# Two-layer encoder trunk: w_down sums beside the up projection, w_up sums closer together, last channel block reordered, weights, table load and transposes moved

## The chip, the cores and the metric

The kernel runs on one core of a Trainium2 chip. The metric is the device time of one execution in microseconds (us). Three runs of the kernel before gave 2811.72 to 2815.82 us, with a median of 2812.99. The core has five engines that run side by side and wait for each other through semaphores: TensorE (PE, matrix products), VectorE (DVE), ScalarE (ACT), GpSimd (POOL) and SyncE (SP), which issues most of the DMA transfers. DMAs with an addition on the way (accumulating ones) are issued by POOL.

## What is computed

Two layers (DEPTH = 2) over x of 1024 x 1024, float32. Cut to what matters:

```python
for l in range(DEPTH):
    h = rms_norm(x, mix_norm[l])
    x = x + hybrid_mixer(h, ...)            # 6 MLA heads, 6 GQA heads, gMLP; then @ w_out
    h = rms_norm(x, mem_x_norm[l])
    x = x + memory_cross_attention(h, mem, mem_kv_norm[l], mem_w_q[l], mem_w_kv[l], mem_w_o[l])
    h = rms_norm(x, ffn_norm[l])
    x = x + conv_gated_ffn(h, ffn_w_up[l], ffn_conv_w[l], ffn_conv_b[l], ffn_w_down[l])
return rms_norm(x, final_norm)

def conv_gated_ffn(h, w_up, conv_w, conv_b, w_down):
    a = h @ w_up                            # 1024 -> 2 x 2816
    a = depthwise_conv3(a) + conv_b         # over the tokens
    gate, val = a[..., :D_FF], a[..., D_FF:]
    return (silu(gate) * val) @ w_down
```

memory_cross_attention normalises mem (256 tokens), makes keys and values of it (4 heads of 128) and attends from all 1024 tokens.

## The kernel before, in words

Every float32 product is made of three fp32r products: both operands are split into a high part (rounded to fp32r) and the rest, and `mm3` adds high x high, high x low and low x high (L116, L117, L118). `load` (L106 to L111) fetches a weight block of 128 x 1024 (512 KB) by an SP DMA (L106), rounds it on POOL (L110, or on ACT at L108) and takes the rest on DVE (L111). `split` does the same to a product: ACT L123 and DVE L124, or with a scale L126 and L127. `transpose4` (L140) makes four 128 x 128 transposes on PE. Tiles of 4 KB per partition come from 46 slots `s`; a load is issued when the slot's earlier readers are done.

A layer is a sequence of stages: the input projection (weights w_m, w_kv, w_q, w_a), attention, the output projection w_out, the memory stage, the up projection and the down projection. Times of layer 0 in the trace: attention some 170 to 500 us, memory stage 590 to 700, up projection 710 to 1190, then down until 1400. Layer 1 stands some 1396 us later.

**Attention.** 24 items (12 heads x 2 halves of the tokens), each with four steps: scores on PE (L725, L726 for GQA, `mm3` for MLA), a maximum on DVE (L295), the exponential on ACT (L299), a division by the sum on POOL (L305), transposes on PE (L140) of what L305 wrote, values (L318, L319). The list `extra` hangs further work on an item. `fill` does so for small pieces of PE work.

**The sums.** Up and down projection are done as 2 x 2 block products with 7 instead of 8 products (numbers m = 1 to 7), for which four sums of blocks of each weight are needed (m = 5, 7, 6, 3). They are made in DRAM: `Blocks.copy` copies a piece by an SP DMA (L777, not before the last L305 issued so far), `Blocks.add` adds another piece to it by an accumulating DMA of POOL (L782). Sum 6 adds the finished sum 5 to its copy, sum 3 the finished sum 6. w_up has 6 pieces per sum (UP_PARTS: one of 0.5 MB and five of 1 MB, 23.1 MB in the 24 sums of a layer), w_down has 3 (768 KB and two of 1 MB, 11.5 MB in 12 sums). `u_6_4` is sum 6 of w_up, piece 4; `d_5_0` is sum 5 of w_down, piece 0.

The 24 w_up copies stand at items 0 to 19, each sum 4 items later; the 12 w_down copies stand at items 0 to 18. The 12 w_down sums are issued by `add_later`: one after each of the four heads of the memory keys (L945) and one in each of the nine score steps of the memory attention (L1031).

**Output projection and memory stage.** In the second half of the output projection (t = 0 to 7) each token block gets 24 `mm3` matmuls (`wo_bc`, `wo_a`). After t = 5 the normalised memory rows `mn` are turned by 16 transposes (`mT`). Then come the key weights mem_wk, the values mem_wv, the queries mem_wq with 8 score steps, and mem_wo.

**Up projection.** 22 channel blocks j, 7 products m each, in the order of the list `order` (L1054 to L1057). One product is 12 matmuls (L1123 to L1125). `fetch` issues the load of one 128 x 512 weight tile (256 KB, from in_w_up or a sum u) and `make_w` splits it (ACT L1076, DVE L1077); `fetch` runs FETCH = 9 and `make_w` AHEAD = 4 products before the product. `post` adds the results on DVE (L1143 to L1149; L1149 for m = 4). The gated blocks go to DRAM, where POOL sums them (L1196, g_u).

**Next layer.** `down` pops small steps from the list `todo`, which turn the next layer's normalised input. Layer 1's first weights w_m are loaded at the head of `layer`.

The order on each engine is the program's order where `tc.keep_in_program_order` asks for it, and otherwise that of a scheduler that may hoist instructions.

## Time and profile before

| what | value |
|---|---|
| median of three runs | 2812.99 us |
| profiled execution | 2817.39 us |
| its span | 2815.4 us |
| PE busy | 2742.6 us, 97% |
| DVE busy | 1971.9 us, 70% |
| ACT busy | 1469.9 us, 52% |
| POOL busy | 689.5 us, 24% |
| DMA of SP's queue (q1) | 323.84 MB, 34.3% of 16 engines' span |
| DMA of POOL's queue (q0) | 92.28 MB, 18.2% |

The span is what the profiler recorded between first and last instruction; the profiled execution's time holds 2 us around it. Busy shares are means over all stages. PE is the engine with the largest share, and its idle time is spread over many waits, so the views that list waits and stretches tell more than the shares. The mean granted clock of PE was 0.991 of the full one.

### The profile page before, as it was taken

To read this page: it belongs to the slowest core of one execution; us is meant where nothing else is said; L and a number is where in the kernel's file an instruction comes from. 1 tells how busy PE (TensorE), PEld (TensorE's weight loads), DVE (VectorE), ACT (ScalarE), POOL (GpSimd) and SP (SyncE) were. 2 spreads that over 40 slices of the span, in tenths; PEclk is the share of its full clock that TensorE was granted. 3 is DMA by queue.
4 is the path that set the end of the run, shared out by engine and by line. 5 is a ranking of instruction groups with operands and counts; after the bars stand their busy time and mean duration, and the time that the engine had idled before them with its cause. 6 is when DMAs were issued, how large, how long until landed. Compare 5 with 4: busy or idle time off the path is not lost.

```text
span 2815.4 us, 38016 instructions
## 1 busy us (share of the span) xinstructions
PE 2742.6 (97%) x13648; PEld 2299.2 (82%) x13648; DVE 1971.9 (70%) x2953; ACT 1469.9 (52%) x2836; POOL 689.5 (24%) x696
## 2 busy tenths in 40 slices
PE   9999999989999999999999999999899999999998
PEld 7987788777878888888889877878788788888887
DVE  5479889555597777774445798894566877777744
ACT  4378877223564444553333788872245544445432
POOL 3245666321100000000123356662210000000000
PEclk9999999999999999999999999999999999999999
DMA  4026886245246656785220269951651556657752
GB/s 145 26 76 178 224 220 154 75 120 128 83 124 170 175 164 176 219 269 185 86 62 19 78 186 247 224 140 53 150 121 66 146 169 176 168 171 239 247 187 104
DMA packets 160748, 418.80 MB, mean 149 GB/s; under 512 B 17840, under 2 KB 18480, under 8 KB 146224
## 3 DMA queue, kind: packets, MB, share of 16 engines
q1 hardware_dynamic: 137376, 323.84, 34.3%
q0 software_dynamic: 23040, 92.28, 18.2%
q8 instruction: 107, 1.75, 0.3%
q14 instruction: 81, 0.66, 0.1%
q10 hardware_dynamic: 144, 0.26, 0.0%
HBM read 371.75 MB, written 206.05 MB: 205 GB/s over the span
## 4 chain that ended last, share of the span: by engine, by line
PE 82%; DVE 7%; ACT 4%; DMA 3%; issue 2%; POOL 2%; SPq 0%; POOLq 0%; DVEq 0%; ACTq 0%
PE bank L1236 8%; PE bank L116 7%; PE bank L118 7%; PE bank L117 7%; PE pair L1236 6%; PE bank L140 6%; PE bank L1124 5%; PE bank L1125 5%; PE bank L1123 5%; PE pair L1123 4%; PE pair L1124 4%; PE pair L1125 4%; PE pair L116 2%; PE pair L118 2%; PE pair L117 2%
## 5 line engine op out<-in xcount | busy, mean ns | idle before, releaser
L116 PE MATMUL bank<-s,s 128*128 128x512 f32 (+4 forms) x1124 | 408.2, 364 | 13.3 <-DVE s L124 8.0
L118 PE MATMUL bank<-s,s 128*128 128x512 f32 (+4 forms) x1124 | 405.2, 361 | 5.5 <-DVE s L111 5.0
L124 DVE TENSOR_TENSOR s<-bank,s 128x512 fp32r<-128x512 f32 (+3 forms) x552 | 331.1, 629 | 107.8 <-ACT s L123 105.3
L117 PE MATMUL bank<-s,s 128*128 128x512 f32 (+4 forms) x1124 | 404.0, 359 | 0.0
L123 ACT ACTIVATE s<-bank 128x512 fp32r<-128x512 f32 (+3 forms) x552 | 285.9, 555 | 220.6 <-PE bank L140 135.3
L140 PE MATMUL bank<-ident,s 128*128 128x128 f32 (+1 forms) x2320 | 322.8, 275 | 26.8 <-DVE s L127 13.4
L140 PEld LDWEIGHTS bank<-ident,s 128*128 128x128 f32 (+1 forms) x2320 | 270.6, 140 | 84.7 <-DVE s L127 16.6
L305 POOL TENSOR_SCALAR s<-s,stat 128x1024 f32<-128x1024 f32 x192 | 226.0, 1178 | 221.6 <-DVE stat L304 156.7
L1076 ACT ACTIVATE s<-s 128x512 fp32r<-128x512 f32 x308 | 187.8, 627 | 168.6 <-PE bank L1125 49.8
L1124 PE MATMUL bank<-s,s 128*128 128x512 f32 x704 | 274.8, 390 | 0.7 <-DVE s L209 0.7
L1125 PE MATMUL bank<-s,s 128*128 128x512 f32 x704 | 274.2, 389 | 0.0
L1123 PE MATMUL bank<-s,s 128*128 128x512 f32 x704 | 274.0, 390 | 0.0
L295 DVE TENSOR_REDUCE stat<-pair 128x1 f32<-128x1024 f32 x192 | 233.7, 1217 | 44.3 <-PE pair L726 22.5
L116 PEld LDWEIGHTS bank<-s,s 128*128 128x128 f32 x1124 | 215.6, 192 | 42.9 <-DVE s L124 10.4
L1236 PE MATMUL bank<-s,s 128*128 128x512 f32 (+1 forms) x1068 | 242.7, 387 | 1.6 <-DVE stat L131 1.6
L132 POOL TENSOR_TENSOR stat<-stat,mhalf 128x1 f32<-128x1 f32 (+3 forms) x94 | 85.6, 911 | 643.6 <-DVE stat L131 642.0
L118 PEld LDWEIGHTS bank<-s,s 128*128 128x128 f32 x1124 | 216.8, 193 | 31.7 <-DVE s L111 5.4
L1221 DVE TENSOR_TENSOR s<-s,s 128x512 fp32r<-128x512 f32 x264 | 170.6, 685 | 95.4 <-ACT s L1220 95.0
L117 PEld LDWEIGHTS bank<-s,s 128*128 128x128 f32 x1124 | 216.8, 193 | 24.2 <-DVE s L111 0.2
L1236 PEld LDWEIGHTS bank<-s,s 128*128 128x128 f32 x1068 | 198.7, 188 | 42.3 <-DVE x L1325 1.8
L1220 ACT ACTIVATE s<-s 128x512 fp32r<-128x512 f32 x264 | 153.5, 623 | 144.7 <-DMA s<-g_u 42.2
L299 ACT ACTIVATE s<-pair,stat 128x1024 f32<-128x1024 f32 x192 | 214.8, 1119 | 22.1 <-DVE stat L295 13.3
(181 smaller groups left out, 5512.6 us busy)
## 6 DMA issues: line engine op xcount, KB each, us to landing
s<-u SPq DMA_DIRECT2D x176, 256.0 KB, 4.2
u<-in_w_up SPq DMA_DIRECT2D x40, 1024.0 KB, 9.2
s<-in_w_up SPq DMA_DIRECT2D x132, 256.0 KB, 4.4
g_u<-s SPq DMA_DIRECT2D x88, 256.0 KB, 2.6
s<-g_u SPq DMA_DIRECT2D x88, 256.0 KB, 3.3
s<-d SPq DMA_DIRECT2D x88, 256.0 KB, 3.6
u<-in_w_up POOLq DMA_DIRECT2D x20, 1024.0 KB, 12.4
u<-u POOLq DMA_DIRECT2D x20, 1024.0 KB, 12.0
```

What stands on the lines that cost most here:

```text
L116: nc.tensor.matmul(o, l[0], r[0], start=first, stop=False)
L117: nc.tensor.matmul(o, l[0], r[1], start=False, stop=False)
L118: nc.tensor.matmul(o, l[1], r[0], start=False, stop=last)
L123: nc.scalar.activation(hi, src, AF.Copy)
L124: nc.vector.tensor_tensor(lo, src, f(hi), ALU.subtract)
L140: nc.tensor.transpose(b[:m, j * P : (j + 1) * P], s, ident)
L295: nc.vector.reduce_max(self.nm[:, 0:1], s, axis=AX.X, negate=True)
L305: Item.last = nc.gpsimd.tensor_scalar(p, p, r[:, 0:1], 0.0, ALU.mult, ALU.add)
L1123: nc.tensor.matmul(o, lh, rh, start=k == 0 and m in (1, 5, 6), stop=False, skip_group_check=True)
L1124: nc.tensor.matmul(o, lh, rl, start=False, stop=False, skip_group_check=True)
L1125: nc.tensor.matmul(o, ll, rh, start=False, stop=k == 3, skip_group_check=True)
L1236: nc.tensor.matmul(o, lh[p], rh[q], start=m in (1, 5, 2) and i == 0 and k == 0, stop=i == NP - 1 and k == 2, skip_group_check=True)
```

## The change

It does six things.

- The w_down sums move: `add_later` is no longer called in the memory stage but in the up projection, at product m = 5 of the blocks j = 2 to 13.
- The w_up copies stand at items 0 to 13 of attention instead of 0 to 19 (`n * 14`), the sums 4 items later, so at 4 to 17.
- At t = 5 of the last input projection (w_a), ACT gets an exponential of one column, so that the exponential's table is loaded there.
- The memory transposes are made in four pieces after t = 2, 3, 4, 5 (4 transposes each); the `mT` slots are taken at t = 2.
- The last channel block (j = 21) is done in another order: (21,1), (21,6), (20,4), (21,5), (21,7), (21,2), (21,3), (21,4).
- Layer 1's w_m loads are put into the `todo` list of layer 0's down projection.

```diff
--- before.py
+++ after.py
@@ -381,14 +381,13 @@
             if after:
                 after(t)
 
-    def layer(l, nt, last):
+    def layer(l, nt, w_m, last):
         colt = colts[l]
 
         def col(i, n=1):
             return colt[:, i : i + n]
 
 
-        w_m = [load(a["w_m"][l, u], 1024) for u in range(4)] if l else []
         gv = lpool.tile([P, 256], F32, tag="gv", name="gv")
 
         def proj(t, w, n, per):
@@ -542,6 +541,8 @@
                 qn_ = [head_norm(z, tab[:, T_GQ : T_GQ + 64], tab) for z in zq]
             for j, st in Q_STEPS[t]:
                 qn_[j][st]()
+            if t == 5:
+                tc.keep_in_program_order(nc.scalar.activation(stat()[:, 0:1], mhalf[:, 0:1], AF.Exp))
             if t == 6:
                 turn_q(0, 0)
                 turn_q(0, 1)
@@ -849,7 +850,7 @@
 
         extra, steps = {}, w_u.steps()
         for n, (w, m, i) in enumerate(steps):
-            g = n * 20 // len(steps)
+            g = n * 14 // len(steps)
             extra.setdefault(g, []).append(lambda w=w, m=m, i=i: w.copy(m, i))
             extra.setdefault(g + 4, []).append(lambda w=w, m=m, i=i: w.add(m, i))
         later = deque(sorted(w_d.steps(), key=lambda s: (5, 7, 6, 3).index(s[1])))
@@ -914,13 +915,15 @@
             wo_bc(t, 1, bank())
             wo_a(t, 1, bank())
             nt.rows(t)
+            if t == 2:
+                mT = [[sl.get() for _ in range(2)] for _ in range(2)]
+            if 2 <= t < 6:
+                k = 2 * (t - 2)
+                b = transpose4([mn[t_][:, (k + j) * P : (k + j + 1) * P] for j in range(2) for t_ in range(2)])
+                for j in range(2):
+                    hi, lo = (mT[i][k // 4][:, (k % 4 + j) * 256 : (k % 4 + j + 1) * 256] for i in range(2))
+                    split(b[:, j * 256 : (j + 1) * 256], hi, lo, scale=col(C_MEMKV + k + j))
             if t == 5:
-                mT = [[sl.get() for _ in range(2)] for _ in range(2)]
-                for k in range(0, KT, 2):
-                    b = transpose4([mn[t_][:, (k + j) * P : (k + j + 1) * P] for j in range(2) for t_ in range(2)])
-                    for j in range(2):
-                        hi, lo = (mT[i][k // 4][:, (k % 4 + j) * 256 : (k % 4 + j + 1) * 256] for i in range(2))
-                        split(b[:, j * 256 : (j + 1) * 256], hi, lo, scale=col(C_MEMKV + k + j))
                 sl.put(*mn)
         put2([w_o[1, u] for u in range(4)])
         put2(yT)
@@ -942,7 +945,6 @@
                 mm3(b[:, :256], cols(wk[h], k * P, P), memT(k, 0, 256), k == 0, k == KT - 1)
             split(b[:, :256], *cols(kmT, h * 256, 256))
             sl.put(*wk[h])
-            add_later()
             nt.turn(0, range(2 * h, 2 * h + 2))
         bv = [bank(), bank()]
         for u in range(4):
@@ -1028,7 +1030,6 @@
                 m_query(*seq[i + 1], 0)
             if i < len(seq):
                 m_score(*seq[i])
-            add_later()
             if i == len(seq):
                 mob = [pair(), pair()]
                 project_part(mob[:1], [0], range(3), True, False)
@@ -1052,9 +1053,9 @@
             return z[:, i * CH : (i + 1) * CH]
 
         order = [(j, m) for m in (1, 2, 5, 6, 3, 7, 4) for j in range(2)]
-        for j in range(2, NF):
+        for j in range(2, NF - 1):
             order += [(j, 1)] + [(j - 1, 4)] * (j > 2) + [(j, m) for m in (6, 5, 2, 7, 3)]
-        order.append((NF - 1, 4))
+        order += [(NF - 1, 1), (NF - 1, 6), (NF - 2, 4)] + [(NF - 1, m) for m in (5, 7, 2, 3, 4)]
         wop, fetched, made = {}, iter(order), iter(order)
 
         raws, half = {}, []
@@ -1287,6 +1288,8 @@
                 ns.turn(1, range(0, 4))
                 ns.turn(1, range(4, 8))
                 ns.make(5)
+            if m == 5 and j > 1:
+                add_later()
             if j == 1 and m in (5, 6, 3, 7):
                 ns.make({5: 6, 6: 3, 3: 7, 7: 4}[m])
             for _ in range(1 + (len(todo) > 6)):
@@ -1337,18 +1340,23 @@
                 sl.put(xn, junk)
 
             down(final, final, tail)
-            return None
+            return None, None
         nt = NormT(colts[l + 1][:, C_MIX : C_MIX + 8])
+
+        w_next = []
 
         def first_half(t):
             nt.rows(t)
             if t == TPC - 1:
-                todo.extend(lambda k=k: nt.turn(0, range(k, k + 1)) if k >= 0 else None for n in range(KT) for k in (n, -1, -1, -1))
+                for k in range(KT):
+                    todo.extend([lambda k=k: nt.turn(0, range(k, k + 1)), lambda: None, lambda: None, lambda: None])
+                for u in range(4):
+                    todo.extend([lambda u=u: w_next.append(load(a["w_m"][l + 1, u], 1024))] + [lambda: None] * 2)
 
         down(first_half, nt.rows, None)
         while todo:
             todo.popleft()()
-        return nt
+        return nt, w_next
 
     colts = [cpool.tile([P, N_COLS], F32, name=f"cols{l}") for l in range(DEPTH)]
 
@@ -1381,9 +1389,9 @@
     nt0 = NormT(colts[0][:, C_MIX : C_MIX + 8])
     for t in range(4):
         nt0.rows(t)
-    nt_ = nt0
+    nt_, w_m_ = nt0, []
     for l in range(DEPTH):
-        nt_ = layer(l, nt_, l == DEPTH - 1)
+        nt_, w_m_ = layer(l, nt_, w_m_, l == DEPTH - 1)
```

POOL in layer 0, from the output projection into the key weights of the memory stage, before (L110: rounding of a loaded weight, L132: a norm, L782: sums, d: w_down):

```order
L110 TENSOR_SCALAR s_572_6372<-s_571_6371 128x1024
L132 TENSOR_TENSOR stat<-stat,mhalf 128x1
L782 DMA d_5_0_1645<-in_w_down 128x1536
L132 TENSOR_TENSOR stat<-stat,mhalf 128x1
L110 TENSOR_SCALAR s_593_6528<-s_592_6527 128x1024
L782 DMA d_7_0_1651<-in_w_down 128x1536
L132 TENSOR_TENSOR stat<-stat,mhalf 128x1
L110 TENSOR_SCALAR s_579_6424<-s_578_6423 128x1024
L782 DMA d_5_1_1646<-in_w_down 128x2048
L110 TENSOR_SCALAR s_586_6476<-s_585_6475 128x1024
L782 DMA d_5_2_1647<-in_w_down 128x2048
L110 TENSOR_SCALAR s_600_6582<-s_599_6581 128x1024
```

The same place after the change, where L782 is L783:

```order
L110 TENSOR_SCALAR s_572_6374<-s_571_6373 128x1024
L132 TENSOR_TENSOR stat<-stat,mhalf 128x1 x2
L110 TENSOR_SCALAR s_593_6527<-s_592_6526 128x1024
L132 TENSOR_TENSOR stat<-stat,mhalf 128x1
L110 TENSOR_SCALAR s_579_6425<-s_578_6424 128x1024
L110 TENSOR_SCALAR s_600_6580<-s_599_6579 128x1024
L110 TENSOR_SCALAR s_586_6476<-s_585_6475 128x1024
L110 TENSOR_SCALAR s_603_6598<-s_602_6597 128x1024
```

The sums no longer stand between the roundings. They stand among the gate sums (L1197, before L1196) of the up projection, whose first rows are:

```order
L132 TENSOR_TENSOR stat<-stat,mhalf 128x1 x8
L1197 DMA g_u_0_7786<-g_11_0_7753 128x512
L783 DMA d_5_0_1647<-in_w_down 128x1536
L1197 DMA g_u_0_7808<-g_22_0_7775 128x512
L1197 DMA g_u_0_7797<-g_u_0_7786 128x512
L1197 DMA g_u_0_7819<-g_u_0_7797 128x512
L783 DMA d_5_1_1648<-in_w_down 128x2048
L1197 DMA g_u_1_7787<-g_11_1_7754 128x512
L783 DMA d_5_2_1649<-in_w_down 128x2048
```

POOL in attention of layer 0, around the w_up sum u_6_4, before:

```order
L782 DMA u_6_4_1631<-u_5_4_1625 128x2048
L305 TENSOR_SCALAR s_418_4734<-s_418_4734,stat 128x1024
L305 TENSOR_SCALAR s_421_4773<-s_421_4773,stat 128x1024
L305 TENSOR_SCALAR s_424_4809<-s_424_4809,stat 128x1024
L328 TENSOR_TENSOR s_414_4693<-s_430_4865 64x512
L305 TENSOR_SCALAR s_429_4859<-s_429_4859,stat 128x1024
L305 TENSOR_SCALAR s_433_4898<-s_433_4898,stat 128x1024
L685 TENSOR_SCALAR s_450_5069<-s_167_2106,cols_86 128x512
L782 DMA u_6_5_1632<-u_5_5_1626 128x2048
```

There u_3_4, which reads u_6_4, follows 27 rows behind u_6_4, with 13 divisions L305 in between. After the change:

```order
L783 DMA u_6_4_1633<-u_5_4_1627 128x2048
L783 DMA u_6_5_1634<-u_5_5_1628 128x2048
L305 TENSOR_SCALAR s_372_4226<-s_372_4226,stat 128x1024
L305 TENSOR_SCALAR s_376_4271<-s_376_4271,stat 128x1024
L237 TENSOR_TENSOR s_381_4319<-s_143_1713,s_73_703 128x128
L239 TENSOR_TENSOR s_381_4319<-s_143_1713,s_73_703 128x128
L305 TENSOR_SCALAR s_380_4313<-s_380_4313,stat 128x1024
L132 TENSOR_TENSOR stat<-stat,mhalf 128x8
L328 TENSOR_TENSOR s_352_4015<-s_385_4360 64x512
L305 TENSOR_SCALAR s_384_4354<-s_384_4354,stat 128x1024
L783 DMA u_7_5_1640<-in_w_up 128x2048
L783 DMA u_3_4_1645<-u_6_4_1633 128x2048
```

u_3_4 now stands 11 rows behind u_6_4, with four L305 (one item) in between, and earlier in attention.

DVE at the memory transposes of layer 0, before (L371: output projection added to x, L131 and L147: norm of a row block, L127 with 128x256: rest of a transposed memory block):

```order
L371 SCALAR_TENSOR_TENSOR x_83<-bank,stat,x_83 128x512 x2
L127 SCALAR_TENSOR_TENSOR s_560_6251<-bank,cols_86,s_558_6249 128x256
L131 TENSOR_SCALAR stat<-stat 128x1
L127 SCALAR_TENSOR_TENSOR s_560_6251<-bank,cols_86,s_558_6249 128x256
L147 TENSOR_SCALAR s_557_6241<-x_83,stat 128x1024
L127 SCALAR_TENSOR_TENSOR s_560_6251<-bank,cols_86,s_558_6249 128x256
L127 SCALAR_TENSOR_TENSOR s_561_6252<-bank,cols_86,s_559_6250 128x256 x2
L127 SCALAR_TENSOR_TENSOR s_560_6251<-bank,cols_86,s_558_6249 128x256
L127 SCALAR_TENSOR_TENSOR s_561_6252<-bank,cols_86,s_559_6250 128x256 x2
L111 TENSOR_TENSOR s_573_6373<-s_571_6371,s_572_6372 128x1024
```

After the change:

```order
L371 SCALAR_TENSOR_TENSOR x_80<-bank,stat,x_80 128x512 x2
L127 SCALAR_TENSOR_TENSOR s_557_6145<-bank,cols_86,s_555_6143 128x256
L131 TENSOR_SCALAR stat<-stat 128x1
L147 TENSOR_SCALAR s_554_6135<-x_80,stat 128x1024
L127 SCALAR_TENSOR_TENSOR s_557_6145<-bank,cols_86,s_555_6143 128x256
L371 SCALAR_TENSOR_TENSOR x_81<-bank,stat,x_81 128x512 x2
L127 SCALAR_TENSOR_TENSOR s_557_6145<-bank,cols_86,s_555_6143 128x256
L131 TENSOR_SCALAR stat<-stat 128x1
L147 TENSOR_SCALAR s_559_6184<-x_81,stat 128x1024
L127 SCALAR_TENSOR_TENSOR s_557_6145<-bank,cols_86,s_555_6143 128x256
L371 SCALAR_TENSOR_TENSOR x_82<-bank,stat,x_82 128x512 x2
L127 SCALAR_TENSOR_TENSOR s_558_6146<-bank,cols_86,s_556_6144 128x256
```

The eight L127 stood behind the sixth token block's L371; now two stand behind each of four blocks.

## Rows read from the trace of the kernel before

**Rows 1.** The profile's page: span, and part 1, TensorE (share of the span, instructions)

```profile
span 2815.4 us, 38016 instructions
...
PE 2742.6 (97%) x13648; PEld 2299.2 (82%) x13648; DVE 1971.9 (70%) x2953; ACT 1469.9 (52%) x2836; POOL 689.5 (24%) x696
```

**Rows 2.** What PE waited for in the whole span: us in total, times, longest

```profile
PE bank L140 <- DVE s L127: 13.4, 9, 6.3
PE bank L116 <- DVE s L124: 8.0, 2, 4.0
PE pair L725 <- ACT s L299: 5.7, 6, 1.8
PE bank L118 <- DVE s L111: 5.0, 2, 2.6
...
PE bank L140 <- POOL s L305: 3.7, 5, 1.5
PE pair L1123 <- DVE s L1149: 2.7, 2, 1.4
PE bank L116 <- DVE s L127: 2.6, 2, 1.3
...
PE bank L116 <- POOL s L110: 1.7, 1, 1.7
...
PE pair L117 <- DVE s L111: 1.2, 2, 0.6
```

**Rows 3.** Timeline of PE, 646.5 to 647.2: start, us, instruction, [idle before <-releaser]

```profile
646.97 0.47 PE L140 MATMUL bank<-ident,s 128*128 128x128 f32 x1 [5.10 <-DVE s L127]
```

**Rows 4.** Chain of waits, 600 to 650, in order of time: start, us, what

```profile
611.42 11.11 DMA s<-in_mem_wv
...
625.39 0.80 PE bank L116
...
634.45 9.33 DMA s<-in_mem_wq
```

**Rows 5.** Line L106 (loads), issues in 549 to 553: two mem_wk loads of 512 KB

```profile
DMA to landing us min/median/max: 3.6/3.7/3.7
```

**Rows 6.** Line L782 (sums), issues in 590 to 665: 11 w_down sums

```profile
DMA to landing us min/median/max: 6.5/10.8/16.0
```

**Rows 7.** Table by stretch: us; PE, PEld, DVE, ACT, POOL; PEclk, DMA share, GB/s

```profile
610.00:660.00 50.00, 39.45 (x199) 33.88 (x200) 24.70 (x29) 10.39 (x18) 9.67 (x10) 0.86 0.77 183
2005.00:2055.00 50.00, 37.27 (x193) 31.97 (x192) 25.00 (x28) 10.78 (x19) 10.84 (x11) 0.86 0.80 189
```

**Rows 8.** Table by stretch: end of the dense part of attention; the up projection

```profile
410.00:440.00 30.00, 29.68 (x163) 23.77 (x162) 26.14 (x43) 24.72 (x44) 20.61 (x20) 1.00 1.01 242
920.00:1170.00 250.00, 250.00 (x1100) 205.75 (x1099) 183.38 (x237) 113.45 (x157) 20.53 (x25) 1.00 0.59 167
```

**Rows 9.** The profile's page, part 6, loads of w_up: count, KB each, us to landing

```profile
s<-in_w_up SPq DMA_DIRECT2D x132, 256.0 KB, 4.4
```

**Rows 10.** Line L1076 (ScalarE's split), 800 to 1168: its only idle time ended by a DMA

```profile
  DMA g_u<-s: 0.5, 1
```

**Rows 11.** Tile u (w_up sums), 230 to 440: ns min/median/max, first and last start

```profile
L782 POOL DMA_DIRECT2D u<-in_w_up x11: 793/864/1125, 231.7 to 419.8; - x11
L782 POOL DMA_DIRECT2D u<-u x9: 797/813/1119, 256.4 to 423.5; - x9
...
DMA to landing us min/median/max: 4.6/11.2/17.6
```

**Rows 12.** DMA queues, 312 to 319: packets, MB, share of 16 engines

```profile
q0 software_dynamic: 117, 0.94, 66.5%
q1 hardware_dynamic: 121, 0.89, 34.6%
```

**Rows 13.** Timeline of POOL, 334 to 341

```profile
338.89 1.06 POOL L618 TENSOR_SCALAR s<-s 32x1024 fp32r<-32x1024 f32 x1 [1.28 <-PE bank L140]
```

**Rows 14.** Timeline of ScalarE, 163 to 172

```profile
166.69 1.28 ACT L299 ACT_TABLE_LOAD   x1
```

## The prediction

> **What bounds the kernel.** The page comes first [rows 1]: TensorE (PE) is busy for 2742.6 of 2815.4 us, so the end moves only by what PE stands still, some 73 us with the start and the tail, or works at the lower clock. So the list of what PE waits for is read next [rows 2]. Its largest entries are pairs, one wait in each layer. Three of them lie in the memory stage: 8.0 us before L116 for a VectorE split at L124 (4.0 each), 5.0 before L118 for L111 (2.6 and 2.4), and the long ones before L140 for L127, of which the timeline shows layer 0's as 5.10 [rows 3] and the list layer 1's as 6.3. Together 11.7 us in layer 0 and 12.7 in layer 1.
>
> The split by DVE is only the last link. The chain of waits [rows 4] shows what stands behind it: a weight load issued at 611.42 lands 11.11 us later, and PE goes on at 625.39, 2.9 us after the landing (the splits of POOL and DVE). The load issued at 634.45 takes 9.33, and PE goes on at 646.97 [rows 3], 3.2 us after it. The same 512 KB load alone, before the stage, lands in 3.6 to 3.7 us [rows 5]. In between stand the w_down sums: 11 in this stretch, which land in 6.5 to 16.0 us [rows 6]. The table by stretch adds the clock [rows 7]: 0.86 granted on the mean over the 50 us of either layer in which the waits lie. After each of them PE works for a while at 1.2 instead of 2.4 GHz.
>
> **A. The w_down sums leave the memory stage.** Without them a load takes 3.7 us as in rows 5. The first is then split and ready at 611.42 + 3.7 + 2.9 = 618.0. PE wants it at 625.39 - 4.0 = 621.4, or at 618.8 if the 2.6 before that goes too: no wait. The second is ready at 634.45 + 3.7 + 3.2 = 641.3, and PE arrives at 646.97 - 5.10 = 641.9: just no wait. The 2.6 at L118 is DVE's L111, behind POOL's splits, and those stand in one row with the sums that POOL issues. Gaps gained: 11.7 and 12.7. The clock: 0.14 x 50 = 7.0 us per layer were lost, part of it inside the waits, where it costs nothing; 6 for layer 0, and 5 for layer 1, whose last wait is 1.2 longer. Together 35.4; as both margins are under 1 us I leave 1.4 and take **-34**. Bounds: -24 if the waits go and the clock stays, -38 for all.
>
> What the sums do in their new place: one stands at each channel block from 2 to 13, beside the 256 KB weight loads. A product of 12 matmuls takes 250 / (1100 / 12) = 2.73 us [rows 8]. By the constants AHEAD and FETCH a load is issued 9 products before its use: 5 of them, 13.6 us, until its split, 4 more until PE. It lands in 4.4 us [rows 9], so it may come 9 us later before ScalarE's split (L1076) notices and some 18 before PE does, and the sums of the memory stage lengthened a load by 7.4 (11.1 against 3.7). In 800 to 1168 that split waited for no load: its one wait for a DMA is 0.5 us, for a gate store [rows 10]. Twelve sums need 12 x 0.96 MB x 5 us per MB (worked out under C) = 58 us of DMA in some 212 us, 0.27 on top of the 0.59 of rows 8: 0.86, below 1. On POOL only the gate sums stand behind them, whose readers come in the down projection. Cost: **0**.
>
> **C. The w_up sums are pulled together in attention.** This speaks against the change. Before, 24 sums stood in items 4 to 23; now in items 4 to 17, with their copies in 0 to 13. An item is (423.5 - 231.7) / 15 = 12.8 us [rows 11]. Where both queues are busy, a sum costs all engines 0.665 x 7 / 0.94 = 4.95 us per MB and a copy 0.346 x 7 / 0.89 = 2.72 [rows 12]. Per item the change asks for 24 / 14 = 1.71 sums x 0.96 MB x 4.95 = 8.1, for w_up copies of 23.1 MB / 14 x 2.72 = 4.5 and w_down copies of 11.5 MB / 20 x 2.72 = 1.6: 14.2 us in 12.8. Even before, the stretch 410 to 440 reads a share of 1.01 [rows 8]. The excess of 1.4 over items 4 to 13 is a backlog of 14 us.
>
> PE does not read those sums; POOL does the waiting. u_3_4 waits for u_6_4, which now stands one item ahead instead of over three, and u_3_3 for u_6_3 likewise. POOL is held at the issue until that sum has landed, and behind it stand the L305 scalings, which PE's transposes need: rows 2 hold 3.7 us of such waits already. Landings run from 4.6 over 11.2 to 17.6 [rows 11]. At the median nothing happens, as 12.8 are to be had; at the slowest POOL is held 17.6 - 12.8 = 4.8, of which a pause in POOL's own work, such as the 1.28 in [rows 13], covers a part: 3 us or so at PE, twice per layer. Bounds: 0, and 14 per layer, the whole backlog. I take 5 per layer, **+10** in all, nearer to the slowest landing than to the median because the engines will be full.
>
> The packets of 312 to 319 say how the two kinds share: 117 of the sums' queue against 121 of the loads' [rows 12], about equal turns. The Trainium skill ("DMA: Bandwidth & Descriptors", section "Queues, rings and completion order") has each engine go round the queue rows it has work for and drain a whole packet before it switches. By that rule a longer line of copies would not slow a sum, only the neighbouring sum would, and this part would come out near 0. The trace agrees with the turns, but it has no stretch with sums as dense as the change's.
>
> Where the sums go away, at the end of attention, PE waits 0.6 us in each layer (L117) for a DVE split [rows 2]: **-1.2**, between 0 and -3.
>
> **F. Memory transposes in four pieces.** The 1.3 per layer before L116 for L127 [rows 2] is PE after 16 transposes, with DVE still at the eight L127. In pieces of four beside 24 matmuls each, only the last L127 can be left. **-2.6**, between -2 and -2.6.
>
> **D. The last channel block.** PE waits 1.3 and 1.4 for L1149, DVE's read of (20,4) [rows 2], at (21,6). With (21,6) before (20,4) it need not, and the next writer of that bank pair, (21,7), has the 2.73 us of (21,5) in between. **-2.7**, between 0 (the wait goes to (21,7)) and -2.7.
>
> **E. Layer 1's first weights.** SP's order hardly changes, as the loads stood early already; PE gets 12 more matmuls, 2.7 us, before it wants the third block. The 1.7 for L110 [rows 2] goes: **-1.7**, between +0.5 and -2.
>
> **B. The table load.** It takes 1.28 us on ScalarE just before the first exponential [rows 14], and PE waits up to 1.8 for L299 there [rows 2]. ScalarE has idle time for it earlier, but PE's next product waits for DVE's L127 as well (0.5 in rows 2), and DVE's new order puts a split ahead of that L127. The wait changes its name: **+0.5** for both layers, between +1 and -4.
>
> **The sum.** -34 + 10 - 1.2 - 2.6 - 2.7 - 1.7 + 0.5 = -31.7 against the profiled execution's 2817.4: 2785.7. The median of the runs shown is 4.4 lower (0.16%), so **2781**.
>
> **Rivals.** (1) The pulled-together sums cost nothing: u_6_3 and u_6_4 land near the median and no new POOL wait appears: 2771. For it: each is the first of its pair. Against it: the full DMA. 0.23. (2) They cost the whole backlog, 28 us: 2781 + 18 = 2799, and a few us more at the lower clock. For it speaks 14.2 against 12.8; against it that a backlog need not fall on a sum that POOL waits for. 0.10. (3) The waits close but PE stays at the lower level in the memory stage: 11 us less gained, 2792. Against it: every low stretch here follows a wait. 0.06. (4) The loads of the memory stage are late by themselves and its waits stay: A gains some 2 us instead of 34, 2813. Against it: rows 5. 0.05. (5) **Slower:** the weight loads of the up projection starve. Place: PE's L1123 behind L1076 in blocks 2 to 13. If a load gets no turn while a sum is in flight, it comes up to 13 us late (17.6 - 4.4), which the 18 us of lead still cover; two sums on end make 26 and PE stands 8. It decides from 42 / 24 = 1.8 us per sum on: then A and the small parts are used up and C is left on top. At 8 us per pair, 12 pairs, it is 96 us: 2877. Against it: the turns in rows 12 and a share of 0.86. 0.06. My forecast keeps 0.50.
>
> **Numbers.** Low end 2765: the gains near their bounds and C at nothing (2781 - 10 - 6). High end 2802: the whole backlog and 3 us of clock. What lies outside is (4), (5) and part of (2). A measurement of this kernel tells about 0.2% (5.6 us) from no change. Faster by more: 0.50 + 0.23 + 0.10 + 0.06 = 0.89; within it: 0.05; slower: 0.06.
>
> **What would show it.** Right: no PE wait over 1 us in the memory stage, its loads landing in 3.6 to 5 us, a granted clock above 0.97 there; 12 sums per layer in the up projection with PE unbroken; a DMA share of 0.95 to 1.0 through 230 to 420, and waits of PE on L305 of some 3 us. Wrong: PE waits at L1123 in the up projection, waits on L305 summing to over 15 us in a layer, or the load of mem_wq landing after more than 6 us with no sum beside it.

## The result, and the profile after

The change takes 2796.31 us (median of 6 runs, 2792.72 to 2801.51), the kernel before 2813.48 in the same comparison (6 runs, 2811.72 to 2815.98): a ratio of 0.9938, interval 0.9925 to 0.9951, so 17 us faster. The forecast was 2781 with a range of 2765 to 2802: the right side, inside the range, 15 us too fast, and about half of the gain of 32 that was forecast.

The profiled execution took 2792.72 us against 2817.39, which is 24.7 less. The two profiled executions lie on either side of their medians (3.9 above before, 3.6 below after), so the traces show 7.5 us more gain than the medians do. The sum of the prediction was made against a trace; it said 31.7.

What PE waited for in the changed kernel (us in total, times, longest), the list that answers to [rows 2]; lines of the code from L384 on have moved by up to eight:

```profile
PE bank L140 <- ACT s L327: 6.4, 5, 2.9
PE bank L140 <- POOL s L305: 5.1, 6, 1.3
...
PE bank L118 <- DVE s L127: 4.2, 2, 2.1
PE pair L726 <- ACT s L299: 3.9, 8, 0.7
PE bank L116 <- DVE s L124: 3.8, 4, 1.0
PE bank L140 <- DVE s L127: 2.5, 7, 0.6
...
PE bank L319 <- DVE s L124: 2.1, 1, 2.1
...
PE bank L118 <- DVE s L111: 1.2, 2, 0.6
...
PE bank L116 <- POOL s L110: 0.8, 1, 0.8
...
PE pair L1124 <- DVE s L1152: 0.5, 1, 0.5
```

The long waits of the memory stage are gone: 13.4 at L140 for L127 have become 2.5, 8.0 at L116 for L124 are 3.8, 5.0 at L118 for L111 are 1.2. The 2.6 at the memory transposes (L116 for L127) has no line any more. The 2.7 at the last channel block is down to one wait of 0.5, the 1.7 for L110 to 0.8. In their place stand waits that were small or missing before: 6.4 at L140 for L327 and 2.1 at L319 for L124, both in attention, and 4.2 at L118 for L127, at the two places where the table load had stood.

The table by stretch, with the columns of [rows 7]: the two stretches of the memory stage, and the dense part of attention in layer 0.

```profile
610.00:660.00 50.00, 48.40 (x277) 41.51 (x277) 32.65 (x41) 18.10 (x41) 7.98 (x7) 1.00 0.19 56
2005.00:2055.00 50.00, 48.34 (x253) 40.45 (x253) 30.35 (x40) 18.72 (x47) 5.09 (x5) 1.00 0.10 32
230.00:420.00 190.00, 179.17 (x1004) 144.99 (x1003) 164.51 (x286) 156.30 (x317) 115.34 (x112) 0.99 0.99 252
```

In the memory stage the granted clock is 1.00 (0.86 in [rows 7]) and PE is busy 48.4 and 48.3 of 50 us. In attention the DMA engines are full, 0.99 over 190 us.

The loads of the memory stage (L106, issued between 590 and 656), two of which took 11.11 and 9.33 us before [rows 4]:

```profile
DMA to landing us min/median/max: 3.4/3.7/4.9
```

The traces add up as follows. A stage is taken from its first matmul to the first of the next stage; attention ends with its last value matmul. Us, layer 0 and layer 1:

| stage | before | change | difference |
|---|---|---|---|
| attention | 365.3, 363.8 | 368.7, 371.6 | +3.4, +7.8 |
| output projection and memory stage | 240.8, 240.7 | 223.8, 224.6 | -17.0, -16.1 |
| up projection | 429.0, 430.4 | 428.3, 428.3 | -0.7, -2.0 |
| down projection of layer 0 to attention of layer 1 | 362.6 | 362.1 | -0.4 |
| start to attention of layer 0 | 163.6 | 164.2 | +0.6 |

By this count attention of layer 0 runs from 164 to 529 us before and the up projection from 770 to 1199; the times given with the description of the kernel are rougher.

So the expected place gave the gain, and attention gave 11 us of it back.

How attention loses them is seen at its longest wait, in layer 1 (the timeline of the changed kernel: POOL first, then DVE, ACT and PE).

```profile
1736.16 0.80 POOL L783 DMA_DIRECT2D u<-in_w_up  x1
1741.13 0.84 POOL L783 DMA_DIRECT2D u<-in_w_up  x1 [4.17 <-DVE stat L304]
1741.69 1.43 POOL L305 TENSOR_SCALAR s<-s,stat 128x1024 f32<-128x1024 f32 x1
1742.78 2.69 POOL L664 TENSOR_TENSOR s<-s,s 128x1024 f32<-128x1024 f32 x1
1745.17 1.39 POOL L305 TENSOR_SCALAR s<-s,stat 128x1024 f32<-128x1024 f32 x1
1746.25 0.73 POOL L237 TENSOR_TENSOR s<-s,s 128x128 f32<-128x128 f32 x1
1746.67 0.72 POOL L239 TENSOR_TENSOR s<-s,s 128x128 f32<-128x128 f32 x1
...
1742.22 5.34 DVE L236 TENSOR_TENSOR s<-s,s 128x128 f32<-128x128 f32 x1
1747.48 0.28 DVE L238 TENSOR_TENSOR s<-s,s 128x128 f32<-128x128 f32 x1
1747.68 1.21 DVE L295 TENSOR_REDUCE stat<-pair 128x1 f32<-128x1024 f32 x1
...
1748.92 1.11 ACT L299 ACTIVATE s<-pair,stat 128x1024 f32<-128x1024 f32 x1 [4.57 <-DVE stat L295]
...
1750.66 0.98 PE L140 MATMUL bank<-ident,s 128*128 128x128 f32 x4 [2.92 <-ACT s L327]
```

POOL issues u_5_4 at 1736.16. Its next instruction, the issue of u_5_5 (L783), starts only at 1741.13: such a pause of POOL before the issue of a sum is called a hold below. The program's wait there is for the copy of u_5_5, which landed long before. The bracket names L304, which merely ended last before it; other holds have L124 there, or nothing ("issue"). The five instructions that follow run without a pause until 1747.39. DVE's L236 starts at 1742.22, a 128 x 128 product of two tiles in SBUF that takes about 0.3 us elsewhere (L238 below it: 0.28), and ends after 5.34 us, when POOL's row of work has ended. L295 is late by that, the exponential L299 waits 4.57 us for it, ACT's L327 stands behind L299, and PE waits 2.92 us. In layer 0 the same happens at 299.73 and 357.02 (L236 with 3.20 and 3.60 us).

What held the issue at 1741.13 is shown by the sum issued three sums earlier, u_3_2 at 1722.37:

```profile
DMA to landing us min/median/max: 18.4/18.4/18.4
```

It landed at 1722.37 + 18.45 = 1740.82, 0.31 us before. There are three holds above 0.3 us in attention of each layer of the change: at u_7_2 (3.9 and 1.9 us), u_3_3 (0.3 and 1.1) and u_5_5 (2.4 and 4.2). Those at u_7_2 and u_5_5 all end 0.31 us after the third sum back (the one issued three sums earlier) has landed. Those at u_3_3 end 0.39 us after it; there the third sum back is u_6_3, which u_3_3 reads, so the program itself waits for it. PE's waits right behind the holds add up to 9.0 us, where its idle time in attention grew by 11.2.

### The profile page after: what moved, and what is told of

Its sections match the earlier page's. It is cut to its first block, busy times and chain, and to the rows that moved or that the text cites. A ratio compares the mean times of both kernels' runs of the same rounds, so it can differ in the third digit from the quotient of the medians.

```text
span 2790.7 us, 37974 instructions
## 1 busy us (share of the span) xinstructions
PE 2732.1 (98%) x13648; PEld 2289.4 (82%) x13648; DVE 1966.8 (70%) x2953; ACT 1469.7 (53%) x2838; POOL 688.0 (25%) x696
## 4 chain that ended last, share of the span: by engine, by line
PE 84%; DVE 6%; ACT 4%; issue 2%; POOL 2%; DMA 1%; SPq 0%; POOLq 0%; DVEq 0%; ACTq 0%
PE bank L1237 8%; PE bank L116 7%; PE bank L118 7%; PE bank L117 7%; PE pair L1237 6%; PE bank L140 6%; PE bank L1125 5%; PE bank L1126 5%; PE bank L1124 5%; PE pair L1124 4%; PE pair L1125 4%; PE pair L1126 4%; PE pair L116 2%; PE pair L118 2%; PE pair L117 2%; PE bank L319 2%
## 5 line engine op out<-in xcount | busy, mean ns | idle before, releaser
L116 PE MATMUL bank<-s,s 128*128 128x512 f32 (+4 forms) x1124 | 405.1, 360 | 5.6 <-DVE s L124 3.8
L124 DVE TENSOR_TENSOR s<-bank,s 128x512 fp32r<-128x512 f32 (+3 forms) x552 | 330.8, 630 | 106.1 <-ACT s L123 103.4
L118 PE MATMUL bank<-s,s 128*128 128x512 f32 (+4 forms) x1124 | 400.0, 357 | 5.4 <-DVE s L127 4.2
L117 PE MATMUL bank<-s,s 128*128 128x512 f32 (+4 forms) x1124 | 399.0, 355 | 0.3 <-DVE s L111 0.3
L140 PE MATMUL bank<-ident,s 128*128 128x128 f32 (+1 forms) x2320 | 327.8, 275 | 22.8 <-ACT s L327 6.4
L140 PEld LDWEIGHTS bank<-ident,s 128*128 128x128 f32 (+1 forms) x2320 | 272.4, 140 | 84.2 <-ACT s L327 12.2
L1077 ACT ACTIVATE s<-s 128x512 fp32r<-128x512 f32 x308 | 187.4, 627 | 181.5 <-PE bank L1126 46.6
L305 POOL TENSOR_SCALAR s<-s,stat 128x1024 f32<-128x1024 f32 x192 | 224.5, 1176 | 217.1 <-DVE stat L304 152.9
L1124 PE MATMUL bank<-s,s 128*128 128x512 f32 x704 | 273.8, 389 | 0.0
L295 DVE TENSOR_REDUCE stat<-pair 128x1 f32<-128x1024 f32 x192 | 233.8, 1218 | 45.9 <-PE pair L727 27.1
L116 PEld LDWEIGHTS bank<-s,s 128*128 128x128 f32 x1124 | 212.4, 189 | 33.9 <-DVE s L124 5.6
L132 POOL TENSOR_TENSOR stat<-stat,mhalf 128x1 f32<-128x1 f32 (+3 forms) x94 | 82.2, 875 | 634.7 <-DVE stat L131 633.1
L118 PEld LDWEIGHTS bank<-s,s 128*128 128x128 f32 x1124 | 212.3, 189 | 31.1 <-DVE s L127 5.1
L1237 PEld LDWEIGHTS bank<-s,s 128*128 128x128 f32 x1068 | 198.7, 188 | 42.3 <-DVE x L1328 1.8
L117 PEld LDWEIGHTS bank<-s,s 128*128 128x128 f32 x1124 | 212.6, 189 | 23.8 <-DVE s L111 0.6
L299 ACT ACTIVATE s<-pair,stat 128x1024 f32<-128x1024 f32 x192 | 214.9, 1119 | 26.1 <-DVE stat L295 22.1
```

What stands on the lines that cost most here:

```text
L116: nc.tensor.matmul(o, l[0], r[0], start=first, stop=False)
L117: nc.tensor.matmul(o, l[0], r[1], start=False, stop=False)
L118: nc.tensor.matmul(o, l[1], r[0], start=False, stop=last)
L124: nc.vector.tensor_tensor(lo, src, f(hi), ALU.subtract)
L140: nc.tensor.transpose(b[:m, j * P : (j + 1) * P], s, ident)
L295: nc.vector.reduce_max(self.nm[:, 0:1], s, axis=AX.X, negate=True)
```

## The experiments

**The sums of attention back in place (e1_keep20).** The change, without its closer w_up sums.

```diff
-            g = n * 14 // len(steps)
+            g = n * 20 // len(steps)
```

> The change with the w_up sums of attention back on items 4 to 23 (copies on 0 to 19). Theory (the closer sums cost the attention of the change some 11 us in its two layers: POOL is held at the issue of a sum, its work then bunches and holds up DVE): about 2785 us, attention back to 364 to 366 us per layer, DVE's L236 never above 1.5 us, no wait of PE over 1.5 us between 230 and 420. Rival (the attention lost by the new order of the other instructions, or by the earlier table load): 2796, long L236 still there.

2784.7 us (2783.96 to 2785.48), ratio to before 0.9894, interval 0.9881 to 0.9906: 11.6 faster than the change (8.4 between the profiled executions), as the theory said. Attention takes 367.0 and 364.2 us, L236 at most 1.35. A pause of POOL of another kind is left. The table by stretch, then POOL and PE in the timeline, and the landing of the w_out load issued at 436.6:

```profile
230.00:440.00 210.00, 204.94 (x1162) 167.75 (x1160) 184.47 (x327) 179.79 (x361) 129.39 (x125) 1.00 0.86 222
410.00:470.00 60.00, 56.29 (x313) 46.04 (x312) 49.77 (x79) 46.11 (x82) 36.30 (x37) 0.97 0.76 179
...
450.95 1.05 POOL L110 TENSOR_SCALAR s<-s 128x1024 fp32r<-128x1024 f32 x1 [7.85 <-DMA s<-in_w_out]
...
459.96 0.33 PE L140 MATMUL bank<-ident,s 128*128 128x128 f32 x1 [2.58 <-POOL s L305]
...
DMA to landing us min/median/max: 14.2/14.2/14.2
```

A load of w_out, behind the last copies in SP's queue and on full engines (which of the two counts was not separated), lands in 14.2 us, POOL stands 7.85 us at its split L110, four L305 come late, and PE waits 2.58 us and has 0.97 of its clock in that stretch.

**The closer sums alone (e2_only_c).** The kernel before with `n * 14`.

> The kernel before with the closer w_up sums alone. Theory: slower by the 11 us that attention lost in the change, so about 2824; memory stage unchanged with its six long waits. In attention two POOL holds of 2 to 5 us per layer, each at the sum that is issued while three others are still under way, ending 0.3 us after the oldest of them lands. Rival (closer sums are harmless by themselves): 2813.

2830.87 us (2829.4 to 2833.41), ratio 1.0058, interval 1.0045 to 1.0070: 18 slower than before. The closer sums cost by themselves, more than the 11 expected. In the trace attention is 371.3 and 372.4 us long, 6.0 and 8.6 more than before. POOL and DVE, timeline:

```profile
352.98 0.80 POOL L782 DMA_DIRECT2D u<-in_w_up  x1
357.51 0.81 POOL L782 DMA_DIRECT2D u<-in_w_up  x1 [3.73 <-DVE s L124]
...
359.03 4.88 DVE L236 TENSOR_TENSOR s<-s,s 128x128 f32<-128x128 f32 x1
```

The hold (3.73 us, at u_5_5) and the long L236 behind it (4.88) are there, without any other part of the change. The hold at u_7_2 (299.30) is 3.16 us long, with an L236 of 2.50.

**The w_down sums alone (e3_only_a).** The kernel before with `add_later()` taken out of the memory stage and put at m = 5 of blocks 2 to 13.

> The kernel before with the w_down sums moved to the up projection and nothing else. Theory: the memory stage gains what the change showed there less the transposes' 2.6, so 33.1 - 2.6 = 30.5 us: about 2783, below the change itself since attention stays as before. Rival (the move also costs attention or the up projection): 2794 or more.

2785.96 us (2781.83 to 2790.61), ratio 0.9901, interval 0.9886 to 0.9915: 27 faster, near the 30.5 expected, and by itself a better kernel than the whole change. In the trace the two memory stages are 15.4 and 14.0 us shorter, attention 1.9 and 0.6, but the up projection of layer 0 is 5.3 longer, which I had put at nothing (that of layer 1 is 1.1 shorter). What ACT waited for there:

```profile
ACT s L1161 <- DMA g_u<-s: 4.8, 1, 4.8
```

ACT's convolution step (L1161) waits 4.8 us for a store of a gated block, whose slot it reuses; DVE and then PE are late by it (PE waits 2.3 us for L1139 and 1.6 for L1147, where before has no such wait). In the whole change ACT's wait is 1.4 us.

**Without the early table load (e4_no_b)** and, later, the same on the best kernel **(e12_k17_no_b).** The line with `AF.Exp` at t = 5 is left out.

> The change without the one-column exponential, so that the table load falls again just before attention's first exponential. Theory (the wait only changes its name): within 2 us of the change, 2796, PE waiting 1.8 for L299 plus 0.5 for L127 at 170 in place of 0.4 plus 2.1. Rival (the early load is worth its 1.28 us per layer): 2799.

> The run with the w_up sums on items 4 to 20, without the one-column exponential, so that the table load falls just before attention again. Theory (that part of the change is worth 0 to 2 us, as the run without it showed on the change itself): 2771 to 2774. Rival (it costs, since the split of a loaded weight now stands ahead of the one PE waits for): 2768 to 2770, a better kernel without it.

2798.14 us (2796.38 to 2799.58) against 2796.31 with it, and 2773.8 (2772.2 to 2774.43) against 2771.6: 2 us worse without it both times, less than one comparison can tell. The wait did change its name: in e12 it is 1.8 at L299 and 0.5 at L127, in the change 0.4 and 2.1. If the 2 us are real, the term of +0.5 had the wrong sign.

**Between 14 and 20 items (e5_k17, e9_k16, e10_k15).** The change with `n * 17`, `n * 16` and `n * 15`.

> The change with the w_up sums on items 4 to 20 (copies on 0 to 16), between the change (4 to 17) and the run on items 4 to 23. By the DMA account of the prediction an item asks for 24/17 x 0.96 x 4.95 = 6.7 for sums, 23.1/17 x 2.72 = 3.7 for copies and 1.6: 12.0 us in 12.8. Theory (the cost begins where the DMA has no room): no hold of POOL, 2784 to 2786. Rival (cost grows evenly with density): halfway, about 2790.

> The change with the w_up sums on items 4 to 19 (copies on 0 to 15). The DMA account gives 7.1 + 3.9 + 1.6 = 12.6 us per item in 12.8. Theory (POOL is held only where the third sum back has not landed, which needs a full DMA): no hold, 2771 to 2775, like the run on 4 to 20. Rival (the cost grows evenly from 17 to 14 items): 2780.

> The change with the w_up sums on items 4 to 18 (copies on 0 to 14). The DMA account gives 7.6 + 4.2 + 1.6 = 13.4 us per item in 12.8: a backlog of 0.6 x 11 = 6 us per layer. Theory: one or two holds per layer, each ending 0.3 us after the third sum back has landed, between the two: 2777 to 2790. Rival (the step comes with the pairs of sums that 14 gives, not with the full DMA): 2771 to 2775.

| spread of the copies | us (median) | ratio to before, interval | holds of over 0.3 us in attention, layer 0 / 1 |
|---|---|---|---|
| 14 (the change) | 2796.31 | 0.9938 [0.9925, 0.9951] | 3 / 3 |
| 15 | 2782.78 | 0.9895 [0.9881, 0.9910] | 1 / 1 |
| 16 | 2777.04 | 0.9877 [0.9862, 0.9891] | 0 / 0 |
| 17 | 2771.60 | 0.9852 [0.9831, 0.9873] | 0 / 0 |
| 20 | 2784.70 | 0.9894 [0.9881, 0.9906] | 0 / 0 |

17 is the best, 25 us below the change and 13 below 20, which none of the accounts had said. Holds of over 0.3 us come only at 14 and 15. The one at 15 (2.1 and 1.3 us) is at u_6_2, which reads u_5_2, the third sum back, so the program's own wait falls together there with the landing that the theory goes by. And 15, which fell into its range of 2777 to 2790, is not slower than 16 by its holds alone: in the traces its attention is 0.5 shorter in layer 0 and 2.7 longer in layer 1, its up projections 1.5 and 2.3 longer, with a granted clock of 0.76 from 776 to 783 and from 2158 to 2165, where 16 has 1.00. At 15 the DMA engines are also as full as in the change (0.99 from 230 to 420), and PE is busy 184.24 us there against 179.17, so it is not the full engines that take the change's time.

At 17 the copies, and all sums but the last, also end by the time the w_out load is on its way. Stretch, landing of the w_out load issued at 435.1, and waits of PE:

```profile
410.00:470.00 60.00, 59.70 (x339) 49.03 (x337) 54.33 (x88) 49.76 (x90) 41.09 (x40) 1.00 0.54 118
...
DMA to landing us min/median/max: 3.5/3.5/3.5
...
PE bank L118 <- DVE s L127: 4.2, 2, 2.1
...
PE bank L140 <- POOL s L305: 2.0, 4, 0.8
```

The load lands in 3.5 us instead of 14.2, POOL is not held at L110, and PE is busy 59.70 of 60 us where it was 56.29 at 20. So the spread has a cost at either end. At 16 the time is 5 us above that at 17, out of the expected 2771 to 2775, and no hold of over 0.3 us explains it: its trace shows a wait of 1.5 us at L140 for L305 in either layer, which is there at 20 as well and not at 17, and two short stretches at the lower clock (0.79 from 389 to 397 and from 1990 to 1998). Why the order of POOL's work falls better at 17 was not followed further.

**Full engines without holds (e6_full_no_hold).** On e1_keep20, every w_up copy is made a second time into memory that nothing reads.

```diff
                 c = nc.sync.dma_start(self.sum[m, i], self.piece(...))
+                if len(self.parts) == 6:
+                    z = dpool.tile(...)
+                    c = nc.sync.dma_start(z, self.piece(...))
```

> The run with the w_up sums on items 4 to 23, with every w_up copy made twice, the second into memory that nothing reads (23 MB per layer more). DMA demand per item 5.7 + 2 x 3.1 + 1.6 = 13.5 us in 12.8: full engines, but one to two sums under way at a time, so no hold of POOL. Theory (POOL's hold is what costs attention, not the full DMA): about 2785 to 2788. Rival (full engines cost by themselves, by late loads and slower sums): 2795 or more.

2850.28 us (2842.15 to 2853.72): as a number this falls to the rival (2795 or more), but its price lies in another place than the full stretch. The table by stretch, the wait of POOL and that of PE, and the landing of the w_out load issued at 455.2:

```profile
230.00:440.00 210.00, 204.99 (x1151) 167.83 (x1150) 183.02 (x324) 178.47 (x358) 127.63 (x123) 0.99 1.00 272
440.00:490.00 50.00, 22.31 (x115) 17.93 (x114) 18.70 (x28) 15.02 (x28) 12.79 (x15) 0.70 0.75 224
...
479.68 1.04 POOL L110 TENSOR_SCALAR s<-s 128x1024 fp32r<-128x1024 f32 x1 [31.86 <-DMA s<-in_w_out]
...
483.34 0.48 PE L140 MATMUL bank<-ident,s 128*128 128x128 f32 x1 [21.57 <-POOL s L305]
...
DMA to landing us min/median/max: 24.4/24.4/24.4
```

From 230 to 440 the engines are full (1.00), and PE is busy 204.99 us, against 204.94 in e1_keep20 with a share of 0.86. Full engines alone cost nothing there. The loss comes behind it, by the late loads that the rival also named: SP's queue holds copies that take 30 to 50 us to land, the w_out load lands in 24.4 us, POOL stands 31.9 us at its split, PE 21.6, and the clock of the next 50 us is 0.70.

**Five sums on end (e7_group).** On e1_keep20, `extra.setdefault(4 * (g // 4) + 7, ...)` for the sums, whose order is that of 5, 7, 6, 3, so that none in a group reads another of it.

> The run with the w_up sums on items 4 to 23, with the sums of four items issued together (about five on end, each independent of the others in its group; copies in the same order). The DMA has as much to do as there, but more than three sums are wanted at once. Theory (POOL cannot issue a fourth 1 MB sum before the oldest of three has landed, and stands): the fourth sum of a group starts 0.3 us after the first has landed, the fifth 0.3 us after the second; POOL held 8 to 12 us per group, PE waits of several us for L305 behind each, 5 groups and two layers: 2810 to 2840. Rival (POOL's queue takes more sums than that, and the holds of the change had another cause): five issues about 0.6 us apart, 2785 to 2790.

2886.80 us (2884.65 to 2888.75), ratio 1.0262. The first group of layer 0 on POOL, the landing of its first sum, and what PE waited for L305 in the whole span:

```profile
271.94 2.71 POOL L783 DMA_DIRECT2D u<-in_w_up  x3
280.42 0.83 POOL L783 DMA_DIRECT2D u<-in_w_up  x1 [5.77 <-issue]
286.18 0.81 POOL L783 DMA_DIRECT2D u<-in_w_up  x1 [4.93 <-DVE stat L304]
...
DMA to landing us min/median/max: 8.2/8.2/8.2
...
PE bank L140 <- POOL s L305: 48.7, 21, 8.2
```

Three issues stand together (x3). The first of them lands at 271.94 + 8.2 = 280.2, the fourth is issued at 280.42, 0.25 us after it by the unrounded times. The second lands at 285.93, and the fifth is issued at 286.18. The theory's rule held in every group; the price was higher than its 2810 to 2840.

**Halves (e8_halves).** The change with each w_up sum as two DMAs of half the columns.

```diff
-                nc.gpsimd.dma_start(self.sum[m, i], src, accum_op=ALU.add)
+                for o in range(0, self.parts[i] * CH, n):
+                    nc.gpsimd.dma_start(self.sum[m, i][:, o : o + n], src[:, o : o + n], accum_op=ALU.add)
```

> The change with every w_up sum issued as two DMAs of half the size. If POOL's limit is a number of DMAs (three), half as much data is under way, POOL is held at most sums: slower than the change, 2805 or more. If it is an amount of data (3 MB), six halves may be under way and the holds stay where they were, at the third sum before: about the change plus POOL's 0.5 to 1 us more per sum, 2796 to 2802.

2948.45 us (2943.07 to 2950.86), ratio 1.0478: it is the number that is limited. The first four halves, each 256 or 512 KB, the landing of the first, and the waits for L305:

```profile
231.81 2.70 POOL L785 DMA_DIRECT2D u<-in_w_up  x3
242.00 0.85 POOL L785 DMA_DIRECT2D u<-in_w_up  x1 [7.48 <-issue]
...
DMA to landing us min/median/max: 9.9/9.9/9.9
...
PE bank L140 <- POOL s L305: 118.2, 30, 8.4
```

The fourth is issued at 242.00, 0.25 us after the first landed (231.81 + 9.9). A half lands in 11.7 us at the median in layer 0, a whole sum of the change in 17.0, so a half takes well over half as long, and twice as many have to go through. In all 14 traces of this case, 160 or more accumulating DMAs each, none was issued while three earlier ones were still under way. Where POOL was held, the issue starts 0.25 or 0.31 us after the oldest of the three has landed, for 256 KB as for 1 MB; where it also reads that sum, as u_3_3 does, 0.39 or 0.40.

**Twelve w_down sums on end (e11_dense_up).** On e5_k17, `if j > 1` in place of `if m == 5 and j > 1`.

> The run with the w_up sums on items 4 to 20, with the twelve w_down sums issued at each product from block 2 on instead of one per block, so on end. Rival (5) of the prediction at its strongest. With three sums under way all the time the weight loads get about half of the DMA for some 12 x 8.6 = 100 us, where they ask for 0.59: they fall behind by up to 24 us, of which 18 are covered. Theory (the lead covers all but the last of it): 2775 to 2790, waits of PE at the first matmul of a product near blocks 3 and 4. Rival (starved loads): 2850 or more. If the loads keep their turn wholly: 2772.

2820.79 us (2818.66 to 2829.29), against 2771.6: 49 slower, between the theory and its rival. Each up projection is 24 us longer. The wait of ACT and that of PE at its longest, and a later one of ACT, DVE and PE:

```profile
832.03 1.24 ACT L1164 ACTIVATE s<-s,cols 128x1024 f32<-128x1024 f32 x1 [15.66 <-DMA g_u<-s]
...
836.56 0.80 PE L1124 MATMUL pair<-s,s 128*128 128x512 f32 x1 [13.18 <-DVE s L1142]
...
866.33 0.63 ACT L1077 ACTIVATE s<-s 128x512 fp32r<-128x512 f32 x1 [6.74 <-DMA s<-in_w_up]
...
867.00 0.69 DVE L1078 TENSOR_TENSOR s<-s,s 128x512 fp32r<-128x512 f32 x1 [6.75 <-ACT s L1077]
...
868.43 0.47 PE L1124 MATMUL pair<-s,s 128*128 128x512 f32 x1 [2.66 <-DVE s L1150]
```

It was not a weight load that cost most. A store of a gated block took 23.1 us to land (at most 10.5 in e5_k17), ACT's convolution (L1164) had to wait for the store's slot, and PE stood 13.2 us at L1124. The loads were late too (up to 28.2 us, 12.1 in e5_k17), and their lead covered that only in part: ACT waited 6.7 us for one at L1077, DVE behind it at its split L1078, DVE's addition L1150 came late by that, and PE lost 2.7 us; another 2.0 at 885 follow a wait of 6.2 in the same way. So the rival had a share in it.

## Why the prediction was right or wrong

**A and F (-34 and -2.6).** Right in mechanism, a little large. The two stages gained 33.1 us in the traces, where 36.6 were forecast; PE's idle time there fell by 23.3 us (27.0 were listed), which leaves 9.8 for the clock (11 forecast). What is left are waits of 0.6 at L118, 1.0 at L116 and, in layer 1, 0.6 at L140, the places with the small margins. The loads land in 3.4 to 4.9 us, as the sum had them. Alone, A gave 29.5 there (e3_only_a), which leaves 3.6 for F and the rest.

**A in the up projection (0).** The step that weighed only the weight loads failed. With one sum per block the whole change shows no loss there, but e3_only_a loses 5.3 us in layer 0, and e11_dense_up shows the weak place: the stores of the gated blocks, which the argument had not looked at, have less cover than the 18 us of the loads. Weight loads of up to 28 us cost PE some time there too, as rival (5) had it.

**C (+10).** The size was near: attention lost 11.2 in the traces where the terms of C, of the end of attention and of B made 9.3, and taking C back gained 11.6 (e1_keep20). Alone it cost 18 (e2_only_c). POOL was held at a sum, as forecast. But the step that named which sum failed. It was to be u_3_4, waiting for u_6_4: in the trace u_6_4 has landed at 398.4 and u_3_4 goes out at 401.21. Nearly all of the hold time, 12.4 of 13.8 us, was at u_7_2 and u_5_5, which wait for no other sum in the program, and it came from three sums under way. Only the 1.4 us at u_3_3 are the wait that was forecast. The way to PE was another one too: not L305 late, or only in part, but a DVE product held while POOL worked off what had piled up. That the size came out near is therefore luck.

By the Trainium skill ("SBUF — State Buffer", section "Who interferes with whom") a DVE instruction with two inputs in SBUF contends with a GpSimd instruction that reads SBUF, and the one that comes second is blocked while the first runs. The trace agrees: L236 with 5.34 us ended 0.17 us after POOL's last instruction, and the two of layer 0 ended 0.16 us after theirs. It goes further than the Trainium skill in one point: L236 was not let in between five POOL instructions on end.

The rule on turns ("DMA: Bandwidth & Descriptors" of the Trainium skill, section "Queues, rings and completion order") was to leave this part near 0. The trace agrees in part: in layer 0 the copies suffered more (up to 43.7 us to land, 18.3 before) than the sums (up to 24.2, before 17.6). But copies did slow a sum: in e6_full_no_hold, with twice the copies and the same sums as in e1_keep20, the sums issued from 230 to 440 landed in 14.5 us at the median instead of 12.8, and in 24.6 at most instead of 18.6. That a slower sum blocks the fourth one was not in the rule.

**D (-2.7)** came as worked out, as far as is shown: the two up projections are 2.75 shorter, and a wait of 0.5 is left. No run takes D, E or F out alone. **E (-1.7)** gave 0.4: the wait for L110 went from 1.7 to 0.8, and the rest was lost to small waits beside it. **B (+0.5)**: two comparisons point to -2, inside its bounds.

**The end of attention (-1.2).** The sign was right and the reason too narrow. What the later places cost is seen between e1_keep20 and e5_k17: 7.0 and 5.4 us of attention, in layer 0 mostly through the late w_out load, which the prediction had not found; in layer 1 a wait of 1.5 us at L140 for L305 (at 1740) and a short stretch at the lower clock (0.79 from 1772 to 1780) are part of it, and the rest was not followed.

**The whole.** Between traces 31.7 were forecast and 24.7 measured: 3.5 of A and F, 1.3 of E, 1.9 of the attention terms and 0.6 at the start make the difference. The other 8 of the 15 us by which the median was missed lie in the two profiled executions: 4.4 were taken off because before's stood above its median, and the change's own stands 3.6 below.

## What to carry to other kernels

Before packing accumulating DMAs closer, count how many of them are under way at any time: here the fourth one stops POOL, and everything behind it in POOL's order, until the oldest has landed, for 256 KB as for 1 MB. Look also at what is late at either end of such a stretch, since the last copies delay the first load behind them; one figure in the middle (17 instead of 14 or 20) was worth 13 to 25 us. And when a transfer is declared covered, check the stores whose slots are reused as well as the loads.

## What was not expected of the hardware

- Three accumulating DMAs of POOL can be under way; a fourth issue that is held starts 0.25 or 0.31 us after the oldest of the three has landed (0.39 or 0.40 where it also reads that one), for pieces of 1 MB as for halves of them.
- A DVE product of 128 x 128 from two SBUF tiles took 5.34 us beside five POOL instructions on end (its like: 0.28 at the median, at most 1.35 in the kernel before); PE stood 2.92 us by it.
- DMA engines that were full for 210 us (share 1.00) did not slow PE at all (204.99 busy us against 204.94); the price, 21.6 us at PE, came with the load behind them.
